# The forward substitution of the delta rule's 32-row blocks: from VectorE to GpSimd

## The chip, the cores and the metric

The kernel runs on one core of one Trainium2 chip. The metric is the device time of one launch in microseconds (us); lower is better. The engines are TensorE (PE in the profile, PEld for its weight loads), VectorE (DVE), ScalarE (ACT), GpSimd (POOL) and SyncE (SP), which issues the DMAs. Each engine works through its own instructions in the order in which the program lists them.

## The reference, cut to what matters

One encoder layer for 512 prompt tokens and 8 × 16 decode tokens, 640 columns in all. Two branches read one big projection of `x`: a softmax attention with forget gates (FoX) and a gated delta rule. The delta rule works on chunks; each chunk has a triangular system whose matrix is the identity plus a strictly lower triangular part:

```python
lmat = jnp.where(strict, jnp.einsum('nbhid,nbhjd->nbhij', kb, kc) * decay, 0.0)
amat = lmat + jnp.eye(c, dtype=lmat.dtype)
solve = functools.partial(lax.linalg.triangular_solve, left_side=True, lower=True)
u = solve(amat, vc * bc[..., None])
w = solve(amat, kb * jnp.exp(gc)[..., None])
```

The branches are gated, projected, merged, normalised and gated once more. There are 8 delta-rule heads, each with 128-wide keys and values.

## The kernel before, in words

All big products run on TensorE in three passes with weights split into a high and a low part (`wh`, `wl`): ScalarE casts the high part (L326), VectorE subtracts it (L327). One such pair is a "piece" of four k-steps; up to five pieces are held ahead (`PIECES`, L61, L341). `column` (L383) multiplies one weight column with all 640 tokens: 16 k-steps of 6 matmuls of 320 columns (L380, L381). `pair` (L433, matmuls at L458) does two columns with seven products in place of eight.

The stages follow one another: `front`, `phase_fox`, `phase_gdn`, `tail`. `phase_gdn` (L1536) runs, for each of the 8 delta-rule heads, four columns and then some merge-gate columns (`FILL`), then four plain columns and four half pairs of the output projection.

Everything that is not a big matmul is written as Python generators, queued in lanes. After each k-step, `tick` (L124) lets every lane that is due issue its next stretch. When a lane is due is decided while the program is built, by a model: `clock` counts the matmuls, and `saw` (L80) adds for each instruction a duration to the `busy` time of its engine. The constants are in L100: 0.17 us + 0.0011 us per element of a partition for VectorE, 0.21 + 0.00085 for ScalarE, 0.25 + 0.0020 for GpSimd. After `yield n` a generator sleeps for n ticks and until the clock has reached the modelled end of what it issued, plus 0.25 us; after `yield -1` for one tick and until 1.5 us before that end (`watch`, L107).

For each head the delta rule goes through four lanes in turn:

- `gdn` (L877), in the lane `work`: transposes, norms, decay factors, the matrices `lt` and `qk` of five tiles of 128 tokens. It starts only when head h-2 is through its chunks.
- `gdn_blocks` (L962), in the lane `blocks`: the 20 diagonal 32×32 blocks of `lt` go through DRAM (`ld`) into `lanes`, where 80 partitions each hold one block (each block four times, for 8 of its 32 right-hand columns). A loop over 31 columns j then does the forward substitution on `x` (80 × 8 × 32): a product into `tmp` (L978) and a subtraction (L980), each over 8 × (31 - j) elements, with a `yield -1` after every second j. L982 sets the first column once. `x` goes out through SP (L986, to `xd`) and comes back as `u0` (L989). Then the lane waits until head h-1 is through its chunks, loads the decode state (L993) and hands over.
- `gdn_chunks` (L998), in the lane `chunks`: GpSimd copies of padded operands and of `u0` into `uu` (L1003, L1008); the block merge, which begins with VectorE's transpose of `u0` into `m0` (L1102) and the matmuls that read it (L1111); then the recurrence over four chunks (for example L1160, ScalarE's `vn` at L1162, the matmuls at L1165) and the decode step, in which GpSimd makes `vm` (L1072).
- `gdn_out` (L1014), in the lane `ends`: norm and gate of the head's output; for head 7 its transposes (L1037) come shortly before the `tail`, which must wait for them (L1728).

GpSimd has more to do in this stage: `weight_sums` (L271) adds and subtracts weight tiles of up to 171 columns (L292); `strip_evac` (L835) sets and copies the first columns of a convolution strip (L838, L843), behind which ScalarE's first tap (L854) waits; `conv_silu` copies its tails (L849, L850).

Of the kernel before, what the change touches and what calls it, by code (L numbers as in the profile page):

```python
# [14 lines left out]
ALU = mybir.AluOpType  # L15
# [37 lines left out]
class Kernel:  # L53
# [908 lines left out]
    def gdn_blocks(self, h, kq, lt, qk, qg, kt, vr, cs):  # L962

        nc = self.nc
        for a in range(4):
            sl = slice(32 * a, 32 * a + 32)
            nc.sync.dma_start(out=self.ld[:, a].rearrange("t j i -> j t i"), in_=lt[sl, :, sl])
        yield 5
        lanes = self.zt([80, 32, 32], "lanes")
        nc.sync.dma_start(out=lanes.rearrange("p j i -> p (j i)"),  # L970
                          in_=bass.AP(self.ld.tensor, self.ld.offset, [[1024, 20], [0, 4], [1, 1024]]))
        yield 5
        x = self.zt([80, 8, 32], "sx")
        tmp = self.zt([80, 8, 32], "sx2")
        for j in range(31):
            n = 31 - j
            xo = self.eye if j == 0 else x
            nc.vector.tensor_tensor(out=tmp[:, :, 0:n], in0=xo[:, :, j:j + 1].to_broadcast([80, 8, n]),  # L978
                                    in1=lanes[:, j:j + 1, j + 1:32].to_broadcast([80, 8, n]), op=ALU.mult)
            nc.vector.tensor_tensor(out=x[:, :, j + 1:32], in0=xo[:, :, j + 1:32], in1=tmp[:, :, 0:n], op=ALU.subtract)  # L980
            if j == 0:
                nc.vector.scalar_tensor_tensor(out=x[:, :, 0:1], in0=tmp[:, :, 0:1], scalar=0.0,  # L982
                                               in1=self.eye[:, :, 0:1], op0=ALU.mult, op1=ALU.add)
            if j % 2 == 1:
                yield -1
        nc.sync.dma_start(out=self.xd, in_=x.rearrange("p c i -> p (c i)"))  # L986
        yield 5
        u0 = self.zt([P, 5, 32], "u0")
        nc.sync.dma_start(out=u0, in_=bass.AP(self.xd.tensor, self.xd.offset, [[32, P], [4096, 5], [1, 32]]))  # L989
        while self.chdone < h - 1:  # L990
            yield 2
        st = self.zt([P, 8, P], "st")
        nc.sync.dma_start(out=st, in_=self.i["st"][h])  # L993
        yield 8
        self.bdone = h
        self.chunks["gens"].append(self.gdn_chunks(h, kq, lt, qk, qg, kt, vr, cs, u0, st))
# [1445 lines left out]
```

## Time and profile before

| what | value |
|---|---|
| median of 3 runs | 2189.33 us (2188.91 to 2189.61) |
| span of the profiled execution, first to last instruction | 2185.3 us |
| busy PE / DVE / ACT / POOL | 2168.4 / 1555.4 / 924.8 / 317.7 us |
| DMA, mean over the span | 193 GB/s |
| granted TensorE clock, mean | 0.999 |

The page lists no device time of its own for the profiled execution. The median of the runs lies 4.0 us above its span, for what lies before the first and behind the last instruction. A busy PE means that at least one matmul was under way; the records of matmuls overlap. Idle time in a group of instructions stands behind the bar, with the event that ended it.

### The profile page before, as it was taken

What the parts mean: (1) busy time and instruction counts of PE and PEld (TensorE: products, weight loads), DVE (VectorE), ACT (ScalarE), POOL (GpSimd) and SP (SyncE); (2) the same over time, 40 slices, a digit from 0 to 9 for tenths busy, and PEclk for the clock granted to TensorE, in tenths of its full rate; (3) what the DMA queues carried; (4) which work ended last, traced back from release to release, by engine and by line L of the source; (5) the groups of instructions that cost most, each with busy time, mean ns of one, the idle gap of its engine ahead of it and who ended that gap; (6) DMA issues with size and microseconds to landing.
All of it is one profiled execution on the core that took longest, in us unless ns stands there. A gap on an engine that the chain in (4) does not pass through costs nothing. (4 is left out here: it accounts for less than half of the span.)

```text
span 2185.3 us, 41804 instructions
## 1 busy us (share of the span) xinstructions
PE 2168.4 (99%) x15606; PEld 2101.9 (96%) x15606; DVE 1555.4 (71%) x3194; ACT 924.8 (42%) x2058; POOL 317.7 (15%) x542
## 2 busy tenths in 40 slices
PE   9999999999999999999999999999999999999998
PEld 7799999999999999999999999999999999999998
DVE  6877677667455456676776867767757787789987
ACT  4344444444333345334434535435434343354544
POOL 0022323333111101111121211210000000011100
PEclk9999999999999999999999999999999999999999
DMA  6356665666888857844535444436567656673475
GB/s 233 104 183 198 201 190 185 196 198 212 319 293 282 303 190 246 289 115 132 151 115 148 133 117 145 135 116 190 174 213 256 220 168 205 195 270 137 149 229 172
DMA packets 222283, 421.12 MB, mean 193 GB/s; under 512 B 33768, under 2 KB 118840, under 8 KB 222080
## 3 DMA queue, kind: packets, MB, share of 16 engines
q1 hardware_dynamic: 222080, 418.45, 58.9%
q8 instruction: 123, 2.02, 0.4%
q14 instruction: 80, 0.66, 0.1%
HBM read 323.29 MB, written 95.07 MB: 191 GB/s over the span
## 5 line engine op out<-in xcount | busy, mean ns | idle before, releaser
L327 DVE TENSOR_TENSOR wl<-wr,wh 128x512 fp32r<-128x512 f32 x638 | 442.4, 703 | 287.6 <-ACT wh L326 281.4
L326 ACT CAST wh<-wr 128x512 fp32r<-128x512 f32 x638 | 389.9, 618 | 317.8 <-PE g L381 137.7
L380 PE MATMUL g<-xh,wh 128*128 128x320 f32 (+1 forms) x1184 | 385.1, 325 | 0.2 <-ACT xh L354 0.2
L380 PE MATMUL g<-xl,wh 128*128 128x320 f32 (+1 forms) x1184 | 366.0, 309 | 0.3 <-DVE xl L355 0.3
L381 PE MATMUL g<-xh,wh 128*128 128x320 f32 x1184 | 366.0, 309 | 0.0
L381 PE MATMUL g<-xl,wh 128*128 128x320 f32 x1184 | 365.7, 309 | 0.0
L380 PE MATMUL g<-xh,wl 128*128 128x320 f32 (+1 forms) x1184 | 365.7, 309 | 0.0
L381 PE MATMUL g<-xh,wl 128*128 128x320 f32 x1184 | 365.5, 309 | 0.0
L458 PE MATMUL g<-xh,wh 128*128 128x320 f32 (+1 forms) x1072 | 334.0, 312 | 2.3 <-ACT m L1241 1.6
L458 PE MATMUL g<-xl,wh 128*128 128x320 f32 (+1 forms) x1072 | 332.0, 310 | 0.6 <-DVE xl L355 0.6
L458 PE MATMUL g<-xh,wl 128*128 128x320 f32 (+1 forms) x1072 | 332.0, 310 | 0.0
L292 POOL TENSOR_TENSOR ws<-ws 128x171 f32<-128x171 f32 (+2 forms) x184 | 135.5, 736 | 771.9 <-DMA ws<-in_w 763.3
L380 PEld LDWEIGHTS g<-xh,wh 128*128 128x128 f32 x1184 | 223.0, 188 | 12.3 <-issue 8.0
L381 PEld LDWEIGHTS g<-xh,wh 128*128 128x128 f32 x1184 | 223.1, 188 | 0.9
L380 PEld LDWEIGHTS g<-xl,wh 128*128 128x128 f32 x1184 | 222.8, 188 | 0.9 <-DVE xl L355 0.9
L380 PEld LDWEIGHTS g<-xh,wl 128*128 128x128 f32 x1184 | 222.4, 188 | 0.2 <-DVE wl L327 0.2
L381 PEld LDWEIGHTS g<-xl,wh 128*128 128x128 f32 x1184 | 222.6, 188 | 0.0
L381 PEld LDWEIGHTS g<-xh,wl 128*128 128x128 f32 x1184 | 222.3, 188 | 0.0
L458 PE MATMUL g<-t,wh 128*128 128x320 f32 (+1 forms) x976 | 216.6, 310 | 0.0
L458 PEld LDWEIGHTS g<-xh,wh 128*128 128x128 f32 x1072 | 201.8, 188 | 4.1 <-ACT m L1241 2.1
L458 PEld LDWEIGHTS g<-xl,wh 128*128 128x128 f32 x1072 | 201.6, 188 | 1.2 <-DVE xl L355 1.1
L458 PEld LDWEIGHTS g<-xh,wl 128*128 128x128 f32 x1072 | 201.9, 188 | 0.0
(443 smaller groups left out, 3594.4 us busy)
## 6 DMA issues: line engine op xcount, KB each, us to landing
wr<-in_w SPq DMA_DIRECT2D x259, 512.0 KB, 4.1
kc<-in_kc SPq DMA_DIRECT2D x32, 512.0 KB, 6.4
vc<-in_vc SPq DMA_DIRECT2D x32, 512.0 KB, 6.9
ws<-in_w SPq DMA_DIRECT2D x96, 128.0 KB, 3.5
md<-m SPq DMA_DIRECT2D x32, 320.0 KB, 3.3
t<-md SPq DMA_DIRECT2D x32, 320.0 KB
sr<-in_w SPq DMA_DIRECT2D x18, 512.0 KB, 3.6
ws<-in_w SPq DMA_DIRECT2D x100, 85.5 KB, 2.5
```

The source lines that it names most:

```text
L292: nc.gpsimd.tensor_tensor(out=o, in0=x, in1=y, op=op)
L326: nc.scalar.copy(out=hi, in_=src)
L327: nc.vector.tensor_tensor(out=lo, in0=src, in1=hi.bitcast(F32), op=ALU.subtract)
L380: nc.tensor.matmul(ps[0], whl[w], xhl[o][:, a], start=(first and x == 0), stop=(last and x == 2))
L381: nc.tensor.matmul(ps[1], whl[w], xhl[o][:, b], start=(first and x == 0), stop=(last and x == 2))
L458: nc.tensor.matmul(ps, a[:, w], b, start=(k == 0 and n == 0 and not more), stop=(k == last and n == 2), skip_group_check=True)
```

## The change

In the loop of `gdn_blocks`, the product and the subtraction are issued by GpSimd in place of VectorE. The instruction that sets the first column, once per head, becomes a plain copy on GpSimd; it does not read `tmp` any more. Nothing else in the text changes. As `saw` books the instructions on GpSimd's modelled time, the places where the lanes issue can move.

```diff
         for j in range(31):
             n = 31 - j
             xo = self.eye if j == 0 else x
-            nc.vector.tensor_tensor(out=tmp[:, :, 0:n], in0=xo[:, :, j:j + 1].to_broadcast([80, 8, n]),
+            nc.gpsimd.tensor_tensor(out=tmp[:, :, 0:n], in0=xo[:, :, j:j + 1].to_broadcast([80, 8, n]),
                                     in1=lanes[:, j:j + 1, j + 1:32].to_broadcast([80, 8, n]), op=ALU.mult)
-            nc.vector.tensor_tensor(out=x[:, :, j + 1:32], in0=xo[:, :, j + 1:32], in1=tmp[:, :, 0:n], op=ALU.subtract)
+            nc.gpsimd.tensor_tensor(out=x[:, :, j + 1:32], in0=xo[:, :, j + 1:32], in1=tmp[:, :, 0:n], op=ALU.subtract)
             if j == 0:
-                nc.vector.scalar_tensor_tensor(out=x[:, :, 0:1], in0=tmp[:, :, 0:1], scalar=0.0,
-                                               in1=self.eye[:, :, 0:1], op0=ALU.mult, op1=ALU.add)
+                nc.gpsimd.tensor_copy(out=x[:, :, 0:1], in_=self.eye[:, :, 0:1])
             if j % 2 == 1:
                 yield -1
```

## The prediction, made before the change was run

> **What bounds the kernel now.** I read the page's busy times first, then TensorE's time in stretches, then whom TensorE waited for, always for the stage in which the substitution runs (from about 950 to 1590 us).
>
> ```profile
> span 2185.3 us, 41804 instructions
> PE 2168.4 (99%) x15606; PEld 2101.9 (96%) x15606; DVE 1555.4 (71%) x3194; ACT 924.8 (42%) x2058; POOL 317.7 (15%) x542
> ```
>
> The span lies 4.0 us under the median of the runs (2189.33); I take this remainder as unchanged, so a change of the span is a change of the time. TensorE is idle for 2185.3 - 2168.4 = 16.9 us in all. The next view gives the stage itself in stretches (us, busy time of each engine, granted clock, DMA share).
>
> ```profile
> core 0: us, PE busy (x) PEld busy (x) DVE busy (x) ACT busy (x) POOL busy (x), PEclk, DMA share, GB/s
> 1030.00:1110.00 80.00, 80.00 (x615) 77.22 (x614) 58.06 (x166) 35.44 (x102) 14.96 (x37) 1.00 0.48 139
> 1430.00:1510.00 80.00, 78.67 (x556) 75.97 (x555) 53.71 (x168) 33.69 (x97) 8.39 (x18) 1.00 0.44 134
> 940.00:1670.00 730.00, 727.68 (x5484) 703.25 (x5483) 523.60 (x1440) 315.35 (x863) 105.64 (x252) 1.00 0.49 150
> ```
>
> At full clock TensorE is never idle in a usual stretch of 80 us and loses 2.3 us in 730. Overlapping records could hide small losses, so I look at the distance of two matmuls six places apart, one k-step of a column:
>
> ```profile
> 959.93 0.31 PE L380 MATMUL g<-xl,wh 128*128 128x320 f32 x1
> 960.82 0.31 PE L380 MATMUL g<-xl,wh 128*128 128x320 f32 x1
> PE s L1152 <- DVE S L1170: 1.2, 1, 1.2
> PE s L1165 <- ACT vn L1162: 0.8, 1, 0.8
> PE g L458 <- DVE fx L467: 0.2, 1, 0.2
> ```
>
> That is 0.89 us for six, about 0.148 us each, close to the kernel's own 0.88 us per step. The last three rows are all that TensorE waited for in this stage. So TensorE bounds it, and VectorE, at 524 of 730 us, does not. Work taken from VectorE can give back at most these 2.3 us, 0.1%. I count 0.2% (4.4 us) as what a measurement of this kernel can tell from no change. The question is only whether the new work on GpSimd makes TensorE wait.
>
> **The change part by part: what it removes.** Per head 62 products and subtractions and one first-column instruction leave VectorE.
>
> ```profile
> 950.00:1590.00 640.00, 76.39 (x248) 1.00 0.47 140
> 950.00:1590.00 640.00, 74.74 (x248) 1.00 0.47 140
> 962.33 0.41 DVE L978 TENSOR_TENSOR sx<-eye,lanes 80x248 f32<-80x248 f32 x1 [0.55 <-DMA lanes<-ld]
> 994.52 0.17 DVE L980 TENSOR_TENSOR sx<-sx,sx 80x8 f32<-80x8 f32 x1
> 1530.31 0.41 DVE L978 TENSOR_TENSOR sx<-eye,lanes 80x248 f32<-80x248 f32 x1 [0.70 <-DMA lanes<-ld]
> 1576.88 0.17 DVE L980 TENSOR_TENSOR sx<-sx,sx 80x8 f32<-80x8 f32 x1
> ```
>
> The first two rows are VectorE's busy time in L978 and in L980: 151.1 us over eight heads, 18.9 per head. But from the first product to the last subtraction a head takes 32.4 us (first) to 46.7 us (last), because VectorE does its other work between. Removing 151 us of VectorE's time gives nothing directly: the cover is TensorE itself, which is busy throughout.
>
> **What it adds.** GpSimd gets 62 two-input instructions per head of 248 down to 8 elements per partition: 2 × 8 × (1 + ... + 31) = 7936 elements, 128 on average. The trace has no such instruction of this shape; its nearest rows are:
>
> ```profile
> L292 POOL TENSOR_TENSOR ws<-ws x184: 481/730/3800, 119.5 to 1452.8; 128x171 f32<-128x171 f32 x100, 128x256 f32<-128x256 f32 x64, 128x169 f32<-128x169 f32 x20
> L364 POOL TENSOR_TENSOR xl<-lngb,xh x16: 194/258/1327, 1943.9 to 1969.3; 128x2 fp32r<-128x2 f32 x16
> L1072 POOL TENSOR_TENSOR vm<-vnd,cb x8: 612/614/810, 1018.1 to 1600.8; 128x256 f32<-128x256 f32 x8
> L292 POOL TENSOR_TENSOR ws<-ws 128x171 f32<-128x171 f32 x80 | 49.9, 624 | 101.6 <-DMA ws<-in_w 97.0
> L292 POOL TENSOR_TENSOR ws<-sb,ws 128x256 f32<-128x256 f32 x32 | 34.1, 1065 | 2.8 <-DMA sb<-in_w 0.4
> L850 POOL COPY tails<-strip x24: 197/204/451, 861.5 to 1438.7; 128x24 f32<-128x24 f32 x24
> L849 POOL COPY tails<-strip x24: 179/186/457, 861.4 to 1438.5; 128x3 f32<-128x3 f32 x24
> ```
>
> From the minima, 194 ns at 2 elements and 481 at 171 give 1.70 ns per element; the line puts 256 at 626, and L1072, with both inputs broadcast, took 612. So broadcasting costs nothing here. Neither do short rows: 8 rows of 3 elements (L850) cost 18 ns more than 3 elements (L849). At 128 elements the line gives 408 ns, so 62 × 0.408 = 25.3 us per head undisturbed. In this stage L292's 171-wide form takes 624 on average, 143 above the minimum. One such delay:
>
> ```profile
> 964.62 0.40 DVE L980 TENSOR_TENSOR sx<-sx,sx 80x232 f32<-80x232 f32 x1
> 965.47 0.80 DVE L980 TENSOR_TENSOR sx<-sx,sx 80x224 f32<-80x224 f32 x1
> 965.47 2.99 POOL L292 TENSOR_TENSOR ws<-ws 128x171 f32<-128x171 f32 x4
> ```
>
> While GpSimd works, VectorE's subtraction doubles from 0.40 to 0.80 us: the two engines hold each other up. I take 408 + 143 = 551 ns, 34.2 us per head. The ends are 18.9 us (as on VectorE) and 62 × 0.624 = 38.7 us (every size as dear as 171). The first-column copy costs 0.2 us, by L850. I choose 34.2 because it comes from the same stage.
>
> The Trainium skill (GPSIMD Engine Reference, § 3, Performance versus the Vector engine) has GpSimd's elementwise add take 1.96 times VectorE's time, and calls it the wrong engine for such work. By that page an estimate for one head is 18.9 × 1.96 = 37.0 us, 5.3 us over the plan, which by the margins below costs the two tightest heads 0.7 us each; no run here shows one operation on both engines.
>
> **What it moves, and who waits.** The kernel issues the rest of a head by its model: 62 × 0.25 + 7936 × 0.0020 = 31.4 us, with the copy 31.7 us. Only where the real chain is later than planned can TensorE meet an operand that isn't there. By my value GpSimd is 34.2 - 31.7 = 2.5 us late at the end of a head. Behind `x` come the two DMAs on SP, the transpose, and the matmuls of L1111:
>
> ```profile
> SPq L986 <- DVE sx L980: 12.0, 7, 3.3
> xd<-sx SPq DMA_DIRECT2D x8, 80.0 KB, 3.2
> u<-xd SPq DMA_DIRECT2D x8, 80.0 KB, 3.3
> 1003.10 0.30 DVE L1102 STREAM_TRANSPOSE m<-u 128x128 f32<-128x128 f32 x1
> 1006.22 0.44 PE L1111 MATMUL s<-m,lt 32*32 32x32 f32 x16
> 1588.82 0.44 PE L1111 MATMUL s<-m,lt 32*32 32x32 f32 x16
> ```
>
> In the first head the transpose ran as soon as `u0` had landed: 1003.40 - 994.52 = 8.9 us after the last subtraction's start, which is the chain's own length. TensorE took the result 2.8 us later. In the last head the same distance is 1588.82 - 1576.88 = 11.9 us, 3.0 to spare; these are the two tightest of the eight, the others having 4.8 to 7.0, 5.1 on the mean. Besides, SP already waits 12.0 / 7 = 1.7 us for VectorE at L986, so lateness of 1.7 us is covered too. The mean head covers 6.8 us, the tightest 4.5. The 2.5 us are hidden. At 38.7 us, 7.0 late, the two tight heads would lose 2.5 us each: 5 us. While SP waits at L986 the weight loads of L266 queue behind it; five pieces of four k-steps, 17.8 us, cover that.
>
> VectorE loses 18.9 us of work per head and gets delays in return. Its most frequent other instruction is
>
> ```profile
> L327 DVE TENSOR_TENSOR wl<-wr,wh 128x512 fp32r<-128x512 f32 x152 | 106.6, 702 | 91.4 <-ACT wh L326 90.0 <-DMA out_stp<-S 1.1
> ```
>
> of which 152 × 34.2 / 640 = 8 fall beside one substitution. At the 0.4 us seen above these lose 3.2 us per head, and VectorE keeps most of what it gains.
>
> Head 7 sets the end of the stage:
>
> ```profile
> 1645.62 0.60 PE L1037 MATMUL s<-cb,ob 128*128 128x128 f32 x4
> 1651.15 0.31 PE L381 MATMUL g<-xh,wh 128*128 128x320 f32 x1
> ```
>
> Its output transposes run 5.5 us before the tail's first matmul. Its substitution, 46.7 us now, would need 34.2, so this end gets more room.
>
> The sum: -2.3 us at best from TensorE's idle time, about as much again for small new waits, 0 for the rest. **Forecast: 2189.3 us**, its own range 2186.5 to 2193.7, chance 0.74.
>
> **The rivals.**
>
> *GpSimd later than the plan covers (0.08).* The lane's next stretch is issued by the model's 31.7 us; past 31.7 + 6.8 = 38.5 us per head, 0.62 us per instruction, TensorE stands at L1111 in every head. For it speaks the row of 1065 ns for 256 elements, 453 over L1072's 612: contention can be worse than 143. Against it, that is an earlier stage. At 0.75 us, 46.5 us per head, each of eight heads loses 46.5 - 38.5 = 8 us: 64 us, 2253 us.
>
> *ScalarE held at a strip (0.15, slower).* ScalarE's first tap waits for GpSimd's copy, which now queues behind substitutions; ScalarE's next instructions wait too.
>
> ```profile
> ACT cy L854 <- POOL strip L843: 2.6, 2, 1.3
> 1024.99 0.37 ACT L1162 ACTIVATE vn<-s,cs 128x128 f32<-128x128 f32 x1 [2.48 <-PE s L1160]
> 1026.55 0.38 PE L1165 MATMUL s<-vn,kt 128*128 128x128 f32 x2
> ```
>
> This happened twice before, for 2.6 us. The chain of `vn` has 1026.55 - 1025.36 = 1.19 us to spare. The planned part of the queue is known to the plan; the 2.5 us of lateness aren't, and 1.3 us of them would reach TensorE. With about ten strips beside substitutions that is up to 13 us, 2202 us; I price it at 8, 2197. It decides from 1.2 us of lateness with a chunk step right behind the strip. Against it: few strips have one there.
>
> *Faster by more than 4.4 us (0.03).* VectorE, relieved, and a new order of issue could end waits that overlapping records hide. I give 5 us, 2184. Against it stand the 0.89 us per k-step, which leaves nothing.
>
> **How the numbers follow.** Within 0.2%: 0.74. Slower: 0.08 + 0.15 = 0.23. Faster: 0.03. The range leaves out the slow GpSimd and half of the faster rival and takes in the second rival and the row bound of 38.7 us (2194): 2186.5 to 2203.
>
> **What would show it.** VectorE's busy time falls by about 140 us, GpSimd's rises by 8 × 34.4 = 275, to 590; a substitution instruction takes 0.45 to 0.62 us on average; TensorE's idle time from 940 to 1670 stays at 1 to 5 us. A wait of TensorE at L1111 would show the first rival, at L1165 or L1152 behind ScalarE's tap the second. A mean over 0.62 us would make the prediction wrong.

## The result, and the profile after

| | before | after |
|---|---|---|
| median of the runs beside each other | 2189.47 us (4 runs) | 2204.05 us (2202.98 to 2206.11, 4 runs) |
| ratio, 95% interval | | 1.0068 [1.0056, 1.008] |
| span of the profiled execution | 2185.3 us | 2201.2 us |
| granted TensorE clock, mean | 0.999 | 0.996 |

The change makes the kernel 0.7% slower; 2204.05 us lies 1 us above the range. (Lines of the changed kernel behind L982 stand one lower: L1110 is the L1111 of before, L985 the L986.) First the head of the page, the span and each engine's busy time, share and instructions:

```profile
span 2201.2 us, 41834 instructions
PE 2173.3 (99%) x15606; PEld 2106.8 (96%) x15606; DVE 1454.9 (66%) x2690; ACT 926.6 (42%) x2058; POOL 575.1 (26%) x1046
```

TensorE is idle for 2201.2 - 2173.3 = 27.9 us, 11.0 more than the 16.9 of before, and busy for 4.9 us more with the same 15606 matmuls. The two make up the whole difference of the spans, 15.9 us. The three greatest waits of TensorE in the stage (us in all, times, longest):

```profile
PE s L1110 <- DVE m L1101: 8.0, 3, 6.1
PE s L1066 <- DVE og L1037: 1.9, 1, 1.9
PE g L458 <- DVE fx L1700: 1.9, 1, 1.9
```

The greatest stands at the matmuls that read the transposed `u0`, and 6.1 of its 8.0 us fall in one head. (What made the other two waits was not followed back.) That head is head 7, as the timeline shows (start, duration, in brackets the idle time before it):

```profile
1536.98 0.61 POOL L978 TENSOR_TENSOR sx<-eye,lanes 80x248 f32<-80x248 f32 x1 [18.90 <-DMA lanes<-ld]
1577.94 0.21 POOL L980 TENSOR_TENSOR sx<-sx,sx 80x8 f32<-80x8 f32 x1
1578.41 0.30 PE L381 MATMUL g<-xh,wl 128*128 128x320 f32 x1
1584.41 0.31 DVE L1101 STREAM_TRANSPOSE m<-u 128x128 f32<-128x128 f32 x1 [8.15 <-DMA u<-xd]
1584.77 0.64 PE L1110 MATMUL s<-m,lt 32*32 32x32 f32 x16 [6.06 <-DVE m L1101]
1585.78 0.47 PE L381 MATMUL g<-xh,wh 128*128 128x320 f32 x1
```

The substitution ran from 1536.98 to 1578.15, 41.2 us. TensorE came to L1110 at 1584.77 - 6.06 = 1578.71, 0.6 us behind its end, while `u0` needs 6.6 us from that end to go out, come back and be transposed (1584.77 - 1578.15). Behind the wait a big matmul of the same form takes 0.47 us in place of 0.30. The stretches of 2 us show why (columns as before: us, busy times, granted clock, DMA share, GB/s):

```profile
1578.00:1580.00 2.00, 0.72 (x5) 0.46 (x4) 0.00 (x0) 0.00 (x0) 0.86 (x5) 1.00 0.30 57
...
1582.00:1584.00 2.00, 0.00 (x0) 0.00 (x0) 0.00 (x0) 0.00 (x0) 0.00 (x0) 0.51 1.08 368
1584.00:1586.00 2.00, 1.23 (x18) 1.16 (x19) 0.31 (x1) 1.21 (x3) 1.25 (x4) 0.50 1.03 332
1586.00:1588.00 2.00, 2.00 (x9) 2.00 (x9) 0.69 (x1) 0.51 (x2) 0.00 (x0) 0.50 1.00 380
1588.00:1590.00 2.00, 2.00 (x32) 1.63 (x31) 0.64 (x3) 1.27 (x3) 0.00 (x0) 0.78 0.88 300
```

Some 3 us into the wait the granted clock falls to half and comes back about 4 us after work resumes. TensorE's busy time in these stretches, times the part of the clock that is missing, gives some 2 us. The clock fell in the same way behind the two waits of 1.9 us (the last section has the rows); the three places together give 5.1 us, about the 4.9 us of longer busy time. This is the second part of the loss: a wait costs its own length, and sometimes slow matmuls behind it. The Trainium skill (TensorE: Matmul & The Clock Gate, Part 1, What's actually happening) names a half-rate clock after about 3.4 us of idleness; this wait agrees with it, the falls behind waits of 1.9 us do not.

GpSimd's own instructions in the stage (busy us, mean ns | idle before), and who else waited for it:

```profile
L980 POOL TENSOR_TENSOR sx<-sx,sx 80x240 f32<-80x240 f32 (+14 forms) x240 | 128.5, 536 | 18.8
L978 POOL TENSOR_TENSOR sx<-sx,lanes 80x240 f32<-80x240 f32 (+14 forms) x240 | 122.0, 508 | 16.1
L980 POOL TENSOR_TENSOR sx<-eye,sx 80x248 f32<-80x248 f32 x8 | 7.6, 945 | 0.6
L978 POOL TENSOR_TENSOR sx<-eye,lanes 80x248 f32<-80x248 f32 x8 | 6.3, 783 | 40.4 <-DMA lanes<-ld 37.7 <-PE g L381 2.7
```

```profile
SPq L985 <- POOL sx L980: 34.7, 6, 10.6
SPq L985 <- POOL kpad L1002: 20.0, 2, 16.4
ACT cy L854 <- POOL strip L843: 21.5, 8, 5.6
```

An instruction is busy for (128.5 + 122.0 + 7.6 + 6.3) / 496 = 533 ns on average, but 18.8 + 16.1 = 34.9 us of idleness stand before 480 of them, 73 ns each: every instruction needs the result of the one before. From its first product to the end of its last subtraction a head took 36.8 to 46.6 us, 42.3 on the mean: 33.0 us busy in the 62 instructions, 4.5 us idle, and 4.7 us in GpSimd's other work, mostly L292, that stands between them. SP stands at the store of `x` for 34.7 + 20.0 = 54.7 us in eight heads, 6.8 each (1.7 before).

### The profile page after: what moved, and what is told of

It is laid out like the page before. It is cut to its first block, busy times and chain, and to the rows that moved or that the text cites. A ratio compares the mean times of both kernels' runs of the same rounds, so it can differ in the third digit from the quotient of the medians.

```text
span 2201.2 us, 41834 instructions
## 1 busy us (share of the span) xinstructions
PE 2173.3 (99%) x15606; PEld 2106.8 (96%) x15606; DVE 1454.9 (66%) x2690; ACT 926.6 (42%) x2058; POOL 575.1 (26%) x1046
## 5 line engine op out<-in xcount | busy, mean ns | idle before, releaser
L327 DVE TENSOR_TENSOR wl<-wr,wh 128x512 fp32r<-128x512 f32 x638 | 453.8, 721 | 358.3 <-ACT wh L326 355.6
L458 PE MATMUL g<-xh,wh 128*128 128x320 f32 (+1 forms) x1072 | 333.4, 311 | 2.6 <-ACT m L1240 1.6
L458 PE MATMUL g<-xl,wh 128*128 128x320 f32 (+1 forms) x1072 | 332.0, 310 | 0.6 <-DVE xl L355 0.6
L458 PE MATMUL g<-xh,wl 128*128 128x320 f32 (+1 forms) x1072 | 332.1, 310 | 0.0
L292 POOL TENSOR_TENSOR ws<-ws 128x171 f32<-128x171 f32 (+2 forms) x184 | 133.9, 728 | 657.0 <-DMA ws<-in_w 640.4
L458 PE MATMUL g<-t,wh 128*128 128x320 f32 (+1 forms) x976 | 217.0, 311 | 1.9 <-DVE fx L1700 1.9
L458 PEld LDWEIGHTS g<-xh,wh 128*128 128x128 f32 x1072 | 202.0, 188 | 3.6 <-ACT m L1240 2.1
L458 PEld LDWEIGHTS g<-xl,wh 128*128 128x128 f32 x1072 | 201.7, 188 | 1.1 <-DVE xl L355 1.1
L458 PEld LDWEIGHTS g<-xh,wl 128*128 128x128 f32 x1072 | 202.0, 188 | 0.0
```

Of the source, the lines that this page charges most:

```text
L292: nc.gpsimd.tensor_tensor(out=o, in0=x, in1=y, op=op)
L327: nc.vector.tensor_tensor(out=lo, in0=src, in1=hi.bitcast(F32), op=ALU.subtract)
L458: nc.tensor.matmul(ps, a[:, w], b, start=(k == 0 and n == 0 and not more), stop=(k == last and n == 2), skip_group_check=True)
```

## The experiments

Three theories. **A**: the substitution is later than the plan assumed, and nothing else costs anything; the plan issues the consumers of `u0` at its own due time. **B**: GpSimd's traffic costs by itself, since it and VectorE hold each other up. **C** (E in the later texts): the new order of issue costs what it happens to cost, whatever the engine. The table puts all runs beside each other. "Idle" and "busy" are the change of TensorE's idle and busy time against the profile of before. The price is what the plan books for one head's substitution; 31.7 and 15.9 hold the copy of the first column, 38.7 and 42.2 are the 62 instructions alone, for which the first two would be 31.4 and 15.7.

| kernel | price, us | us (runs) | ratio, 95% | idle | busy |
|---|---|---|---|---|---|
| after | 31.7 | 2204.05 (4) | 1.0068 [1.0056, 1.008] | +11.0 | +4.9 |
| e6_half_price | 15.9 | 2292.88 (2) | 1.0472 [1.0451, 1.0493] | +82.7 | +23.1 |
| e1_price | 38.7 | 2189.45 (10) | 1.0001 [0.9992, 1.001] | +1.7 | +1.2 |
| e9_over_price | 42.2 | 2220.37 (4) | 1.0144 [1.0127, 1.016] | +31.8 | +4.8 |
| e10_own_buffer | 42.2 | 2188.55 (10) | 0.9998 [0.9988, 1.0007] | +1.1 | +0.5 |
| e2_old_order | as before | 2201.78 (4) | 1.0062 [1.0045, 1.0079] | +8.7 | +3.6 |
| e7_new_order_dve | 31.7, on VectorE | 2204.14 (4) | 1.007 [1.0055, 1.0085] | +9.9 | +5.5 |
| e5_wait_longer | 31.7 | 2200.28 (4) | 1.0052 [1.0037, 1.0067] | +8.6 | +4.5 |
| e3_last_on_dve | 31.7, 7 heads | 2194.63 (9) | 1.003 [1.0019, 1.004] | +6.5 | +0.5 |
| e4_last_on_pool | 31.7, head 7 | 2193.17 (8) | 1.0022 [1.0012, 1.0033] | +5.0 | +1.3 |

### A dearer price in the plan

```diff
         a, b = ((0.17, 0.0011), (0.21, 0.00085), (0.25, 0.0020))[e]
+        if e == 2 and names[0].startswith(("sx_", "sx2_")):
+            a, b = 0.33, 0.0023
```

> The changed kernel with one thing different: the plan books the substitution's GpSimd instructions at 0.33 us + 0.0023 us per element (38.7 us per head) in place of 0.25 + 0.0020 (31.7 us); the changed kernel took 37 to 47 us. Theory A (the loss is lateness against the plan: the hand-over after the substitution is issued too early, so SP, VectorE and at last TensorE wait): the waits of TensorE behind the transpose of u0 go from 8.0 us to under 2, SP's wait at the store of x falls from 6.8 us per head to about 2, time 2189 to 2194. Theory B (GpSimd beside VectorE and ScalarE is itself the loss, through held SBUF reads and strip copies): 2200 to 2206 as before the edit. Theory C (the order of issue only came to lie badly): anywhere from 2190 to 2204, with waits in other places.

Engine, instructions and data are those of the changed kernel; only the plan knows a dearer price for them. The head of the page and, of TensorE's waits in the stage, the one at the transpose:

```profile
span 2188.2 us, 41825 instructions
PE 2169.6 (99%) x15606; PEld 2102.2 (96%) x15606; DVE 1456.7 (67%) x2690; ACT 926.8 (42%) x2058; POOL 588.6 (27%) x1046
...
PE s L1112 <- DVE m L1103: 0.8, 1, 0.8
```

GpSimd is busy for 588.6 us, more than in the changed kernel, and the loss is gone: 2189.45 against 2189.35 us. So GpSimd's traffic is not a loss by itself, and B falls. The wait at the transpose is down from 8.0 to 0.8 us, SP's waits at the store of `x` from 54.7 to 20.3 us, and ScalarE's 21.5 us behind GpSimd's strip copies are gone.

### The orders and the engines exchanged

The changed kernel with the order of before: the plan books the substitution on VectorE, at VectorE's price.

```diff
+        if e == 2 and names[0].startswith(("sx_", "sx2_")):
+            e = 0
```

> GpSimd does the substitution as in the changed kernel, but the plan books it on VectorE at VectorE's price, so that TensorE, ScalarE and SyncE have exactly the order of instructions of the kernel before. Theory A: the old plan leaves 32 to 47 us for a head (what VectorE needed beside its other work), GpSimd needs 37 to 47; only the heads with short allowances (the first, the sixth) are late, by 5 to 10 us: 2191 to 2198. Theory B: GpSimd's contention is all there, 2202 to 2206. Theory C: the old order is back, 2189 to 2190.

```profile
PE s L1112 <- DVE m L1103: 9.3, 2, 6.9
```

The matmuls that read the transpose are again what waits, and now it is the first head that is late. Its first product and its matmuls:

```profile
962.18 0.61 POOL L980 TENSOR_TENSOR sx<-eye,lanes 80x248 f32<-80x248 f32 x1 [11.60 <-DMA lanes<-ld]
...
1013.07 0.64 PE L1112 MATMUL s<-m,lt 32*32 32x32 f32 x16 [6.94 <-DVE m L1103]
```

In the order of before, this head had 1006.22 - 962.33 = 43.9 us from first product to the use of the result (rows of the prediction); GpSimd needed 1013.07 - 962.18 = 50.9, and the difference, 7.0 us, is the wait. The other wait, 2.4 us, stands in the sixth head. These are the heads that A had named, but the time, 2201.78, lies above A's 2191 to 2198 and almost in B's 2202 to 2206; by the time alone B would fit better, had the dearer price not ruled it out. A had left out the clock, which fell to half behind both waits: TensorE is busy for 3.6 us more. C expected 2189 to 2190 from the order of before and falls as the whole cause: with that order the kernel loses 12.4 us.

The mirror image, substitution on VectorE but planned as if on GpSimd, so that TensorE, ScalarE and SP get the order of the changed kernel:

```diff
+        if e == 0 and names[0].startswith(("sx_", "sx2_")):
+            e = 2
```

> The reverse of the kernel with the old order: VectorE does the substitution as before the change, but the plan books it on GpSimd at GpSimd's price, so that TensorE, ScalarE and SyncE have exactly the order of the changed kernel. Theory A: VectorE needs 32 to 47 us beside its other work and the plan leaves it some 32, as well as less room for VectorE's other work: as slow as the changed kernel or slower, 2200 to 2230, with TensorE waiting behind the transpose of u0. Theory B: no GpSimd contention, 2189 to 2191. Theory C: the bad order is there, 2200 to 2206.

```profile
PE s L1162 <- DVE rp L1158: 3.8, 4, 2.1
PE s L1154 <- DVE S L1172: 2.6, 4, 1.5
...
PE s L1113 <- DVE m L1104: 0.3, 1, 0.3
```

Just as slow as the change (2204.14 us), without one substitution instruction on GpSimd. Here VectorE carries about 19 us per head that the plan has put down to another engine, and VectorE's recurrence steps are late, many small waits in place of one long one; the wait at the transpose, which A expected to see again, is 0.3 us. Of the 5.5 us of longer busy time one fall of the clock, 3.4 us long, gives about 1.4; the rest is not explained. This run alone cannot tell A from C. The two kernels before it can: the order of before is slow, and the dearer price, a new order too, is not.

### More room at the hand-over

```diff
         nc.sync.dma_start(out=self.xd, in_=x.rearrange("p c i -> p (c i)"))
-        yield 5
+        yield 13
```

> The changed kernel with 13 ticks in place of 5 between the store of x and the load of u0, some 7 us more per head between the substitution and the matmuls that use it; the plan's price and SP's early wait at the store of x stay. Theory A, if TensorE's loss is the hand-over alone: its waits behind the transpose fall from 8.0 us to under 2 and the time to 2191 to 2197; if SP's early wait (which holds the weight loads) costs too, 2197 to 2202. Theory B: 2202 to 2206.

```profile
PE s L889 <- DVE kq L867: 6.0, 1, 6.0
PE s L1110 <- DVE m L1101: 2.3, 1, 2.3
```

The wait at the transpose went from 8.0 to 2.3 us, nearly as A has it (under 2), but 6.0 us came up elsewhere, in the convolution of a later head, so that only 3.8 us of 14.6 were won (2204.05 to 2200.28). That is inside A's second range, but not for the reason that A gave. Followed back, `kq` stands in VectorE's order behind steps that wait for ScalarE, and the same strip's first tap on ScalarE had itself waited for GpSimd, whose strip copy stood among the substitution's instructions:

```profile
1311.66 0.85 ACT L854 ACTIVATE cy<-strip,taps 128x664 f32<-128x664 f32 x1 [3.19 <-POOL strip L843]
```

This is the way of the prediction's second rival. How much of the 6.0 us it made, beside the other work of VectorE and ScalarE on the way, is not separated. Room added at one place does not repair a price that is wrong for every instruction.

### One head alone

The first kernel gives head 7 back to VectorE. The second, with `h == 7` in the condition, puts only head 7 on GpSimd.

```diff
+        eng = nc.gpsimd if h < 7 else nc.vector
...
-            nc.gpsimd.tensor_tensor(out=tmp[:, :, 0:n], in0=xo[:, :, j:j + 1].to_broadcast([80, 8, n]),
+            eng.tensor_tensor(out=tmp[:, :, 0:n], in0=xo[:, :, j:j + 1].to_broadcast([80, 8, n]),
```

> The changed kernel, but head 7's substitution (the last of the eight) stays on VectorE; heads 0 to 6 run theirs on GpSimd, and the plan's price for GpSimd (31.7 us per head) is as in the changed kernel. Theory A (GpSimd is later than the plan assumed, and a late head makes TensorE wait at the transpose of u0): the wait of 6.1 us in the last head and the clock lost behind it (about 2 us) go, and so may the small ones just after it, while the lateness of heads 0 to 6 stays; so 8 us off 2204, 2194 to 2198, and SP's wait at L985 stays near 7 us per head. If the cost were spread evenly over the heads (an eighth each, 15/8 = 2 us), 2202. If the mixture only draws another order of issue (E, any new order costs what it happens to cost): anything from 2190 to 2205, with waits at other lines than the transpose's.

```profile
PE s L1067 <- DVE og L1038: 2.3, 1, 2.3
PE g L458 <- ACT ob L1032: 2.2, 1, 2.2
PE s L1111 <- DVE m L1102: 1.4, 2, 0.8
```

2194.63 us: 9.4 of the 14.6 us went with head 7's return. The long wait is gone and TensorE's busy time is back (+0.5 in place of +4.9 us); two waits of 2 us remain, neither at the transpose.

> The mirror image: heads 0 to 6 stay on VectorE, and head 7's substitution alone runs on GpSimd. A: head 7 is 9 us late, as in the changed kernel, and TensorE waits 5 to 7 us behind the transpose of u0 of that head alone, with some 2 us of clock lost behind it; 2196 to 2200. Spread evenly: 2189 + 2 = 2191. E: anything from 2189 to 2200, with no wait at the transpose's line in the last head. GpSimd's busy time should be 318 + 33 = 351 us.

```profile
PE s L1111 <- DVE m L1102: 1.7, 1, 1.7
```

2193.17 us, under A's 2196 to 2200. The wait came where it was expected, but at 1.7 in place of 5 to 7 us. With the other heads on VectorE, this head's substitution took 38.5 us, not 41.2, and the half clock of a long wait did not come. The two parts, 5.6 and 4.2 us by the medians, do not add up to 14.6. With the other seven on GpSimd, head 7's wait is 4.4 us longer, and the slow clock comes behind it; how much of the rest one head hands to the next is not resolved.

### Half the price

```diff
+        if e == 2 and names[0].startswith(("sx_", "sx2_")):
+            a, b = 0.125, 0.0010
```

> The changed kernel, but the plan books a substitution instruction on GpSimd at half its price (0.125 us + 0.0010 us per element, 15.9 us per head in place of 31.7). Engine, instructions and data are as in the changed kernel. A: the rest of a head is issued some 16 us earlier while GpSimd takes what it took, so each head is 16 us later than now, 23 in all, against some 7 us that are covered: 10 to 18 us of TensorE's time per head, 80 to 140 us in eight, and some clock behind each wait: 2290 to 2350; a part of it may be hidden where SP's wait holds other work back in the same way, and then not less than 2240. The waits stand at the transpose of u0. B (contention of the two engines) and E (an order that happens to be bad): 2195 to 2210, as in the changed kernel.

```profile
PE 2191.5 (96%) x15606; PEld 2123.0 (93%) x15606; DVE 1455.3 (64%) x2690; ACT 926.1 (40%) x2058; POOL 571.4 (25%) x1046
PE s L1112 <- DVE m L1103: 55.7, 6, 13.4
PE s L1061 <- DMA st<-in_st: 9.2, 3, 7.1
```

The same work on the same engine, 2292.88 us: within A's range, and 83 us above the top of the others'. The waits stand at the transpose in six heads, and behind the late store on SP the load of the state (`st`) is late too.

### Too dear a price, and a shared buffer

> The changed kernel, with the plan's price of a substitution instruction on GpSimd raised to 0.36 us + 0.0025 us per element, 42.2 us per head (31.7 in the changed kernel). A (only lateness against the plan costs anything): nothing is late any more, even in the last head, which took 41.2 us; 2187 to 2191, no wait of TensorE at the transpose of u0, and SP's wait for the substitution under 10 us in all. E (each new order costs what it happens to cost): as likely as not another 5 to 15 us, 2194 to 2205, with the waits elsewhere.

2220.37 us lies outside both ranges. No wait is left at the transpose, and SP's waits at the store of `x` are down to 11.1 us, but one new wait came, with its releaser on ScalarE:

```profile
PE s L1141 <- ACT x L1137: 30.0, 1, 30.0
ACT x L1137 <- POOL sx L982: 32.6, 1, 32.6
```

Now the plan lets head 6's merge be issued behind the start of head 7's substitution. The merge's `x2` shares the tag `sx2`, with one buffer, with the substitution's `tmp`, and so ScalarE's copy stands until all 62 instructions are through. If that is the cause, a place of its own for `x2` is enough; `t1` uses only 64 of 128 partitions.

```diff
-        t1 = self.t1
+        t1 = self.t1[0:64]
...
-        x2 = self.zt([P, 4, 64], "sx2", 1, "x2")
+        x2 = self.t1
...
-        self.t1 = self.zt([64, 4, 64], "t1")
+        self.t1 = self.zt([P, 4, 64], "t1")
```

> The kernel of the raised price (42.2 us per head), with one edit: x2, the 64-row merge's scratch tile, which shares its single buffer with the substitution's tmp, gets a place of its own in the unused half of t1. A (only lateness and the shared buffer cost anything): the one wait of 30 us at L1141, where head 6's merge stood behind head 7's whole substitution, goes, and nothing else was waiting: 2220 - 30 = 2190, 2187 to 2193. If the wait had another cause (the order that the higher price draws puts head 6's merge behind head 7's substitution for a reason of its own, such as ScalarE's or GpSimd's queue), the wait stays at 20 us or more and the time above 2208.

```profile
span 2186.9 us, 41808 instructions
PE 2168.9 (99%) x15606; PEld 2102.8 (96%) x15606; DVE 1457.3 (67%) x2690; ACT 926.8 (42%) x2058; POOL 581.0 (27%) x1046
PE s L1153 <- DVE S L1171: 0.7, 1, 0.7
PE g L460 <- DVE fx L469: 0.6, 1, 0.6
PE s L1068 <- DVE rp L1064: 0.2, 1, 0.2
```

2188.55 against 2188.70 us, the 30 us are gone and TensorE waits 1.5 us in the stage. So the substitution costs nothing on GpSimd if the plan knows its length and no buffer ties the heads together. It wins nothing either, with VectorE 98 us less busy. No kernel here is measurably faster than before.

### The price of the instructions themselves

> Leaves out the whole computation and measures the substitution's instructions alone, in six stretches one after the other. (1) one substitution on GpSimd, nothing beside it; (2) the same on VectorE; (3) on GpSimd beside 80 VectorE subtractions of 128x512 from SBUF; (4) the same with one input in PSUM; (5) the two kinds in turn; (6) 62 products on GpSimd that do not depend on each other. By the prediction's prices (1) is 62 x 0.408 = 25.3 us and (3) 62 x 0.551 = 34.2 us. By what the changed kernel showed, a gap of 73 ns stands ahead of each dependent instruction, so (1) is 25 + 4.5 = 30 us and (6), without the gap, 26 to 27 us; (2) is 19 us. If the contention is one for SBUF's port between the two engines, (3) is above 35 us and (4) stays at (1)'s time or a little over it; if VectorE's work holds GpSimd up whatever its source, (4) is as long as (3).

The six stretches in the expectation's order (us, then busy PE, PEld, DVE, ACT, POOL, clock, DMA share, GB/s; a stretch runs from first to last instruction):

```profile
6.65:37.66 31.01, 0.00 (x0) 0.00 (x0) 0.02 (x1) 0.00 (x0) 26.23 (x63) 1.00 1.01 390
38.20:58.20 20.00, 0.00 (x0) 0.00 (x0) 17.90 (x64) 0.19 (x1) 0.82 (x2) 1.00 0.23 88
59.32:110.92 51.60, 0.00 (x0) 0.00 (x0) 51.60 (x63) 0.00 (x0) 46.82 (x64) 1.00 0.00 0
121.71:152.78 31.07, 0.00 (x0) 0.00 (x0) 31.07 (x53) 0.00 (x0) 26.29 (x64) 1.00 0.00 1
170.08:218.13 48.05, 0.00 (x0) 0.00 (x0) 48.05 (x77) 0.00 (x0) 43.27 (x64) 1.00 0.00 0
220.78:243.85 23.07, 0.00 (x0) 0.00 (x0) 0.11 (x1) 0.00 (x0) 23.07 (x64) 1.00 0.00 0
```

Alone, GpSimd is busy for 26.2 us (the prediction had 25.3) but takes 31.0: 4.8 us lie between the instructions, 77 ns each. With independent products (last row) they are gone. The plan's 31.7 us is thus the price undisturbed. Beside VectorE subtractions with both inputs in SBUF the same work takes 51.6 us, two thirds more; beside those with one input in PSUM it takes 31.07, as if alone; beside the two kinds in turn, 48.05. The full DMA traffic of the first stretch costs nothing (31.01 us with it, 31.07 without).

## Why the prediction was wrong

**What bounds the kernel, and what VectorE's relief is worth: right.** 98 us less on VectorE (the e10 kernel) moved nothing. In the changed kernel VectorE's busy time fell by 100.5 us, not by 140: of 151.1 us removed, 50.6 came back, about 6.3 per head where the prediction had put 3.2. (With its own 3.2 it should have named 126, not 140.)

**The length of an instruction: right on the mean.** 533 ns against 551, inside the 0.45 to 0.62 us named. In head 7 it was 579.

**The step that failed: "By my value GpSimd is 34.2 - 31.7 = 2.5 us late".** 34.2 us is the sum of the busy times, and a chain of 62 dependent instructions is longer than this sum. The 73 ns between them, 4.5 us per head, were left out. The plan's constant (0.25 us per instruction) was compared with busy times, though it holds these gaps, as the 31.0 us of the undisturbed chain show. With them the chain takes 496 × 533 ns / 8 + 4.5 = 37.6 us, 5.9 late, and SP's wait says 6.8. Put the other way, the plan's 31.7 us is the undisturbed chain, so what is late is the contention: 33.0 us busy per head against 26.2 alone, 6.8. In head 7 the 41.2 us are 35.9 busy in the 62 instructions, 4.4 between them and 0.9 in two copies, 9.5 us over the plan. But this step alone does not explain the result: by the prediction's own covers of 4.5 and 4.7 us in the two tightest heads, 5.9 us of lateness would have cost 2.6 us, 2192, inside the range. And the chain behind the last subtraction, read as 8.9 us long, took 1584.72 - 1577.94 = 6.8 in head 7, so that the cover in before was, if anything, larger than read.

**The second failed step, and the larger: "The mean head covers 6.8 us, the tightest 4.5", and of head 7 "this end gets more room".** The cover was read in the order of before, and the change draws a new order. Head 7 had 1588.82 - 1530.31 = 58.5 us from its first product to L1111 in before (rows of the prediction); in the changed kernel TensorE came to L1110 after 1578.71 - 1536.98 = 41.7 us: it came 10.1 us earlier, and the first product began 6.7 us later, when its `lanes` had landed. That the plan sets this room is shown by the other prices, with the same work on the same engine: 1649.84 - 8.96 - 1603.50 = 37.4 us at half the price, 1578.44 - 0.82 - 1530.60 = 47.0 at 38.7, 1587.82 - 1532.57 = 55.3 at 42.2 with `x2` in its own place, and 1601.85 - 1542.93 = 58.9 with VectorE's price and the order of before (each from that kernel's timeline, a wait taken off). The room that a faster step would leave is room that the plan uses up. So the last head, said to gain room, lost the most: 41.2 + 6.6 us of chain against 41.7. The first head, one of the two tightest before with 43.9 us, had 53.2 and did not make TensorE wait.

**The rivals.** The first, "GpSimd later than the plan covers", is what happened, with the signature that was named (L1111, now L1110), and was given 0.08. It named a wait in every head; it came in three. Its point of decision, 38.5 us per head, was not quite reached by the 37.6 us of the substitution's own instructions and gaps; but it is a mean over heads, and one head at 41.2 with its cover gone sufficed. The second, ScalarE at the strips, is there too (`cy`, 2.6 to 21.5 us) but showed no wait of TensorE at L1165 or L1152; it has a part in the wait for `kq` of e5. A mean over 0.62 us, named as what would prove the prediction wrong, did not come; the prediction watched the wrong number. 37.0 us, the estimate by the Trainium skill's page (GPSIMD Engine Reference, § 3, Performance versus the Vector engine), is nearer to the 37.6 of the trace than the prediction's 34.2. That is luck: alone, the ratio of the two engines was 31.01 / 20.00 = 1.55, not 1.96, and VectorE's work beside it made up the rest.

**What was in no term:** the slow clock behind waits, about 4.9 of the 15.9 us, some 2 of them behind the wait of 6.1 us. The prediction priced a wait at its length alone.

## What to carry to other kernels

Price a chain of dependent instructions by its length from first to last, gaps included, and compare it with a plan's constant only in the same measure. Where a planner sets the order, a cover read in the old trace is not the cover of the new one: ask where the planner will put the consumers once it believes the step to be shorter, and give it a price that holds the contention. Before a step is let run longer beside its neighbours, look which buffers it holds meanwhile.

## What was not expected of the hardware

**The half clock.** In the changed kernel it came behind the wait of 6.1 us, from about 1582 to 1589 us. Short idleness does not decide it by its length alone. The first three rows are the changed kernel behind waits of 1.9 us (L1066), 1.1 (L1110) and 1.9 (L458); the last is the kernel with head 7 on VectorE, in its wait of 2.3 us for the same `og`:

```profile
1090.00:1092.00 2.00, 1.14 (x5) 1.17 (x6) 1.83 (x6) 0.33 (x2) 0.00 (x0) 0.63 0.67 216
1344.00:1346.00 2.00, 1.35 (x22) 1.34 (x23) 1.29 (x3) 1.43 (x5) 1.44 (x2) 1.00 0.81 276
1644.00:1646.00 2.00, 2.00 (x10) 1.96 (x10) 1.33 (x3) 2.00 (x7) 0.00 (x0) 0.50 0.94 268
1092.00:1094.00 2.00, 1.23 (x9) 1.26 (x10) 1.74 (x5) 0.73 (x2) 0.28 (x1) 1.00 0.69 228
```

The clock fell behind the first and the third, and stayed at 1.00 behind the second and, for all its 2.3 us, behind the last. What tells them apart stays open. By the trace's record of the clock, each fall behind a short wait lasted 3.4 us, the one behind 6.1 us twice as long, 6.8.

**Who holds GpSimd up.** Of the two kinds of VectorE instructions tried, only those with both inputs in SBUF do: 51.6 us against 31.07 beside those with one input in PSUM. The Trainium skill (GPSIMD Engine Reference, § 1, Specifications) says that the two engines share their SBUF interfaces and contend where a VectorE instruction has two SBUF inputs; the two stretches agree with it. VectorE pays too: 51.60 / 63 = 0.82 us for an instruction there, against 31.07 / 53 = 0.59 with one input in PSUM.

**The gap.** Dependent instructions on GpSimd stand 73 ns (in the kernel) to 77 ns (alone) behind each other; between independent ones there was no gap (23.07 us, busy throughout).
